# Normalised operands rewritten behind the first product group, second weight parts moved from GpSimd to VectorE, and an instruction planner with a shared port

## The chip, the core and the metric

The kernel runs on one core of a Trainium2 chip. The core has TensorE (matrix products, PE in the profile, with PEld for its weight loads), VectorE (DVE), ScalarE (ACT), GpSimd (POOL) and SyncE (SP), which issues most DMAs. The metric is device time in microseconds: 2119.82 us is the median of three runs before the change (2117.39 to 2120.98). About 0.2% is what a measurement can tell from no change.

## The reference

Everything is float32, with 256 tokens of width 1024. Two blocks of two layers each stand one behind the other.

A layer of the first block is `x += mixer(rms_norm(x))`, then `x += ffn(rms_norm(x))`. Its mixer projects the normalised input into queries, keys, values, gates and a short-convolution branch, runs causal convolutions, evaluates a gated delta rule by chunks (with a triangular solve) in four heads, and projects back. Its feed-forward is `(silu(h Wg) * (h Wu)) Wd` with 2816 hidden columns.

A layer of the second block has three sublayers: feed-forward, token mixer, feed-forward. Each takes

```
rms_norm(x) * gain * (1 + scale) + shift
```

as its input, where scale, shift and an output gate are products of a conditioning vector with `mod_w`, and adds back a gated, normalised result. The token mixer holds a state-space part of 512 channels (a complex scan over time), an attention with forgetting in eight heads, and two sigmoid gates that merge them.

What matters here: each sublayer begins with `rho(t) = 1 / sqrt(mean(x(t)^2) + eps)`, one number for each token, and the first product of `x * gain * rho + shift` with a weight matrix.

## The kernel before, in words

**Layout.** Activations lie transposed: features on the 128 partitions in eight slices (k = 0 to 7), the 256 tokens along the free axis. A product is made at float32 precision from three products of a reduced format: a weight W is cast to a first part `wh` and has a second part `wl = W - wh`, the input likewise `xh` and `xl`, and PSUM gathers `wh xh + wh xl + wl xh` (`group`, line 224, products on line 237). A group is four output slices of 128 columns, eight k-slices and three products each, so 96 products, in four PSUM banks (`pg`, four buffers: the next group's column c has to wait until this group's column c has been read).

**Weights.** They come as a stream of blocks of 128 x 1024 in the order of use (`all_blocks`, `prepare` line 185): SyncE loads one into `wr`, ScalarE or VectorE casts it to `wh` (lines 198, 200), VectorE or GpSimd subtracts `wl` (line 207). A block is two k-slices of a group. Up to four blocks are made ahead. `POOL_SHARE = (1,0,0.56,0)` says which share of the subtractions GpSimd makes, for the stages (first block's mixer, first block's feed-forward, second block's mixer, second block's feed-forward); `HI_SHARE` says the same of casts on VectorE.

**A sublayer.** `pre` (line 345) writes `xh` and `xl` from `x * gain` without rho, so that products can begin before the sum of squares is complete; rho comes later, as a tile of 128 x 256 (line 330 in the first block, line 379 in the second). Every result that leaves PSUM is then multiplied by rho on VectorE (lines 397, 412, 667, 833, 853, 1235, 1328), in the first block's feed-forward a second time on the gate (line 404), and in the first mixer rho is squared and applied to a product (lines 848, 853, 875). In the second block the shift rides along: `xh` has two more columns with the shift vector in two parts, so the `xh` products have 258 columns, and each result column's constant is added up from the two last columns by `shifted` (line 242: VectorE line 245, or ScalarE line 248) and used as a bias.

The feed-forward (`ffn`, line 385) runs six pairs of groups, gate and up, and writes the product of both, split into `ah` and `al`; then the down projection follows in two groups of 22 k-slices. `mixer1` (line 645) runs keys first, then queries, values, and four more groups among the steps of the delta rule (a blockwise solve on lines 783 to 817, where a small product on line 790 alternates with two VectorE steps, 793 and 795). `mixer2` (line 1217) runs `u` first, then seven groups among sixteen pairs of state-space steps (`ssm_pair`, lines 1109 to 1156, on VectorE and GpSimd) and the attention heads.

**GpSimd's other work.** It prepares the state-space tables (`ssm_params`, line 1062), makes three of the eight residual sums at a sublayer's start (lines 570, 571) and multiplies the first two residual slices by `r` ahead of time (`ahead`, line 583; eight slices in the last sublayer). `make` and `ahead` concern the residual of the sublayer's end.

**The order of the work.** The program is written sublayer by sublayer, but what each engine executes is planned: `Order` (line 1549) takes all instructions, gives each an engine, a cost (`price`, line 1583) and dependencies with latencies, lists them by priority in a simulated run (`run`, line 1695), forwards and backwards for several settings, keeps the best list and pins each engine's instructions in its order. In this model engines are independent of one another: a GpSimd instruction and a VectorE instruction run side by side at full speed.

## Time and profile before

| | |
|---|---|
| runs shown (three) | 2117.39, 2119.82, 2120.98 us; median 2119.82 |
| profiled execution, its own time | 2110.74 us |
| its span (first to last instruction) | 2108.9 us |
| TensorE / its weight loads busy | 1929.6 / 1832.8 us (91 / 87%) |
| VectorE busy | 1748.0 us (83%) |
| ScalarE busy | 1044.2 us (50%) |
| GpSimd busy | 654.6 us (31%) |
| mean granted TensorE clock | 0.966 of full speed |
| DMA moved | 391.03 MB, mean 185 GB/s |

The shares are averages over ten sublayers with different limits, so the profile is read by stretches. [...] Matmuls are pipelined and reach into one another, so TensorE's idle time says more than its busy time. An instruction that is held up counts as busy: its duration grows. In a line of the timeline, what stands in brackets is the idle time before it and who ended it.

### The profile page before, as it was taken

What the parts mean: (1) busy time and instruction counts of PE and PEld (TensorE: products, weight loads), DVE (VectorE), ACT (ScalarE), POOL (GpSimd) and SP (SyncE); (2) the same over time, 40 slices, a digit from 0 to 9 for tenths busy, and PEclk for the clock granted to TensorE, in tenths of its full rate; (3) what the DMA queues carried; (4) which work ended last, traced back from release to release, by engine and by line L of the source; (5) the groups of instructions that cost most, each with busy time, mean ns of one, the idle gap of its engine ahead of it and who ended that gap; (6) DMA issues with size and microseconds to landing.
All of it is one profiled execution on the core that took longest, in us unless ns stands there. A gap on an engine that the chain in (4) does not pass through costs nothing. (4 is left out here: it accounts for less than half of the span.)

```text
span 2108.9 us, 38573 instructions
## 1 busy us (share of the span) xinstructions
PE 1929.6 (91%) x14826; PEld 1832.8 (87%) x14826; DVE 1748.0 (83%) x3053; ACT 1044.2 (50%) x1898; POOL 654.6 (31%) x453
## 2 busy tenths in 40 slices
PE   7789999879999998998888879999999888899998
PEld 6789999778999998898666878999999876688997
DVE  8968897887888789977898898877887799977674
ACT  5645644544554555445344454545454534456453
POOL 5532000544300004804666693000000476642000
PEclk9999999989999999999899989999999999999999
DMA  5324777422577777573332546775778432254553
GB/s 200 100 83 139 271 268 283 167 90 91 180 277 272 279 272 250 209 277 125 103 125 80 190 130 209 262 264 187 268 240 280 141 125 90 86 166 145 183 187 120
DMA packets 110248, 391.03 MB, mean 185 GB/s; under 512 B 12912, under 2 KB 13424, under 8 KB 110064
## 3 DMA queue, kind: packets, MB, share of 16 engines
q1 hardware_dynamic: 108336, 382.93, 53.5%
q0 software_dynamic: 1440, 5.24, 0.7%
q8 instruction: 117, 1.92, 0.4%
q14 instruction: 67, 0.55, 0.1%
q10 hardware_dynamic: 288, 0.39, 0.1%
HBM read 383.27 MB, written 1.05 MB: 182 GB/s over the span
## 5 line engine op out<-in xcount | busy, mean ns | idle before, releaser
L237 PE MATMUL g<-xh,wh 128*128 128x258 f32 (+1 forms) x3264 | 933.3, 291 | 42.1 <-DVE xc L667 14.5
L237 PE MATMUL g<-xl,wh 128*128 128x256 f32 x3264 | 934.8, 289 | 10.4 <-DVE xl L360 8.8
L237 PE MATMUL g<-xh,wl 128*128 128x258 f32 (+1 forms) x3264 | 923.7, 288 | 1.7 <-POOL wl L207 0.9
L200 ACT CAST wh<-wr 128x1024 fp32r<-128x1024 f32 (+1 forms) x528 | 550.0, 1046 | 457.3 <-PE g L237 201.5
L207 DVE TENSOR_TENSOR wl<-wr,wh 128x1024 fp32r<-128x1024 f32 (+1 forms) x446 | 575.4, 1298 | 158.8 <-PE g L237 70.2
L237 PEld LDWEIGHTS g<-xh,wh 128*128 128x128 f32 x3264 | 624.6, 193 | 55.5 <-issue 17.2
L237 PEld LDWEIGHTS g<-xl,wh 128*128 128x128 f32 x3264 | 633.1, 194 | 19.0 <-DVE xl L360 11.6
L237 PEld LDWEIGHTS g<-xh,wl 128*128 128x128 f32 x3264 | 627.1, 194 | 5.7 <-issue 3.3
L207 POOL TENSOR_TENSOR wl<-wr,wh 128x1024 fp32r<-128x1024 f32 (+1 forms) x130 | 326.4, 2516 | 642.9 <-PE g L237 239.5
L237 PE MATMUL g<-ah,wh 128*128 128x256 f32 x880 | 249.2, 284 | 3.3 <-DVE act L412 2.5
L237 PE MATMUL g<-ah,wl 128*128 128x256 f32 x880 | 248.1, 283 | 0.0
L237 PE MATMUL g<-al,wh 128*128 128x256 f32 x880 | 247.9, 282 | 0.0
L472 DVE SCALAR_TENSOR_TENSOR mraw<-mraw,siluc 128x1024 f32<-128x1024 f32 x144 | 187.7, 1303 | 20.5 <-DMA mraw<-in_modw 20.0
L237 PEld LDWEIGHTS g<-ah,wh 128*128 128x128 f32 x880 | 166.4, 189 | 3.9 <-issue 3.7
L237 PEld LDWEIGHTS g<-al,wh 128*128 128x128 f32 x880 | 167.0, 190 | 0.0
L237 PEld LDWEIGHTS g<-ah,wl 128*128 128x128 f32 x880 | 165.9, 189 | 0.0
L342 ACT CAST ah<-act 128x256 fp32r<-128x256 f32 x132 | 52.5, 405 | 118.0 <-DVE act L413 93.8
L1109 POOL TENSOR_TENSOR pa<-pa,pb 128x256 f32<-128x256 f32 x96 | 84.6, 897 | 44.2 <-DVE pb L1109 20.6
L1066 POOL COPY stb<-ah 128x1 f32<-128x1 f32 x1 | 0.2, 183 | 224.0 <-ACT ah L342 224.0
L1109 POOL TENSOR_TENSOR pb<-st,stb 128x512 f32<-128x512 f32 x32 | 49.4, 1543 | 56.2 <-DVE st L1134 50.7
L397 DVE TENSOR_TENSOR sg<-g,rho 128x256 f32<-128x256 f32 x132 | 53.9, 420 | 12.6 <-PE g L237 11.2
L1134 DVE TENSOR_TENSOR_SCAN st<-ssm_r,pa 128x128 f32<-128x128 f32 x64 | 63.8, 1015 | 0.2 <-POOL pa L1109 0.2
(451 smaller groups left out, 2749.6 us busy)
## 6 DMA issues: line engine op xcount, KB each, us to landing
wr<-in_wstream SPq DMA_DIRECT2D x568, 512.0 KB, 4.4
mraw<-in_modw SPq DMA_DIRECT2D x144, 512.0 KB, 4.0
stb<-in_ssmb POOLq DMA_DIRECT2D x8, 512.0 KB, 4.7
wr<-in_wstream SPq DMA_DIRECT2D x8, 256.0 KB, 4.5
ux<-gb SPq DMA_DIRECT2D x32, 64.0 KB, 3.2
ux<-gl SPq DMA_DIRECT2D x32, 64.0 KB, 2.4
stb<-in_ssmc POOLq DMA_DIRECT2D x2, 512.0 KB, 5.3
x<-in_x SPq DMA_DIRECT2D x2, 256.0 KB, 4.8
```

The costliest lines, as they stand in the source:

```text
L200: nc.scalar.copy(out=hi[:, :n], in_=raw[:, :n])
L207: e.tensor_tensor(out=lo[:, :n], in0=raw[:, :n], in1=hi[:, :n], op=ALU.subtract)
L237: nc.tensor.matmul(ps[c][:, :x.shape[-1]], wt, x, start=(bi == 0 and k == 0 and i == 0), stop=(bi == len(specs) - 1 and k == n - 1 and i = ...
L342: s.nc.scalar.copy(out=out_h, in_=src)
L397: nc.vector.tensor_tensor(out=a, in0=gp[c][:, :T], in1=rho, op=ALU.mult)
L472: nc.vector.scalar_tensor_tensor(out=w, in0=w, scalar=1.0, in1=s.sc_, op0=ALU.mult, op1=ALU.mult, accum_out=s.mod[l][:, j:j + 1])
L1066: G.tensor_copy(out=flat[:, 0:1], in_=after)
L1109: tt = lambda e, o, a, b, op: e.tensor_tensor(out=o, in0=a, in1=b, op=op)
L1134: scan = lambda i, h, v: V.tensor_tensor_scan(out=st[:, i, h], data0=rb, data1=a4[:, i, h], initial=v, op0=ALU.mult, op1=ALU.add)
```

## The change

It has three parts.

1. **`Input` and `settle`.** `pre` returns an object. The sublayer's first group runs as before with `x * gain` and gets rho (and the shift) on its results. Behind it `settle` rewrites the eight slices of `xh` and `xl` in place with `x * gain * rho + shift`: a product of three on VectorE into `xs` (two buffers), a copy (or an addition of the shift) into `xh` on ScalarE, a subtraction into `xl` on VectorE. All later groups use these, with 256 columns, and their results need no rho and no shift: gates go from PSUM through the activation function on ScalarE, plain results are copied by ScalarE, the up product needs one VectorE instruction. `ahead` is called behind `settle`. In the second block's very first sublayer, where x is scaled by `fing` in place behind `pre`, `settle` uses the plain gains.
2. **`POOL_SHARE = (0,0,0,0)`**: VectorE makes all second parts.
3. **The planner** marks instructions that use a shared port (all of GpSimd's; VectorE's with two wide inputs in SBUF, and copies and scalar operations from SBUF to SBUF) and lets only one of them run at a time; where the port is held, another instruction that needs no port may go first.

```diff
-POOL_SHARE = (1,0,0.56,0)
+POOL_SHARE = (0,0,0,0)
 DEPTH = 2
...
+class Input:
+    def __init__(s, kern, z, gains, shift, xh, xl, rho):
+        s.kern, s.z, s.gains, s.shift, s.xh, s.xl, s.rho = kern, z, gains, shift, xh, xl, rho
+        s.due = True
+    def h(s, k):
+        return s.xh[:, k, :T + 2] if s.due and s.shift is not None else s.xh[:, k, :T]
+    def l(s, k):
+        return s.xl[:, k, :]
+    def settle(s):
+        nc = s.kern.nc
+        s.due = False
+        for k in range(KD):
+            a = s.kern.t(s.kern.misc, [P, T], "xs")
+            nc.vector.scalar_tensor_tensor(out=a, in0=s.z[:, k, :], scalar=s.gains[:, k:k + 1], in1=s.rho,
+                                           op0=ALU.mult, op1=ALU.mult)
+            if s.shift is None:
+                nc.scalar.copy(out=s.xh[:, k, :T], in_=a)
+                nc.vector.tensor_tensor(out=s.xl[:, k, :], in0=a, in1=s.xh[:, k, :T], op=ALU.subtract)
+            else:
+                nc.scalar.activation(out=s.xh[:, k, :T], in_=a, func=AF.Identity, bias=s.shift[:, k:k + 1])
+                nc.vector.scalar_tensor_tensor(out=s.xl[:, k, :], in0=a, scalar=s.shift[:, k:k + 1],
+                                               in1=s.xh[:, k, :T], op0=ALU.add, op1=ALU.subtract)
...
-    def shifted(s, out, ps, scale=1.0):
-        if scale == 1.0:
-            s.nc.vector.tensor_reduce(out=out, in_=ps[:, T:T + 2], axis=mybir.AxisListType.X, op=ALU.add)
-        else:
-            both = s.t(s.misc, [P, 2], "both")
-            s.nc.scalar.activation(out=both, in_=ps[:, T:T + 2], func=AF.Identity, scale=scale, accum_out=out)
+    def shifted(s, out, ps):
+        s.nc.vector.tensor_reduce(out=out, in_=ps[:, T:T + 2], axis=mybir.AxisListType.X, op=ALU.add)
...
         s.make = s.rest = None
-        N = T if shift is None else T + 2
-        return (lambda k: xh[:, k, :N]), (lambda k: xl[:, k, :]), rho, shift is not None
-    def ffn(s, wg, wu, wd, h, done, wg0=0, wu0=0, last=False):
+        return Input(s, z, gains, shift, xh, xl, rho)
+    def ffn(s, wg, wu, wd, h, done, wg0=0, wu0=0, last=False, then=None):
         nc, tc = s.nc, s.tc
-        xh, xl, rho, shift = h
+        rho = h.rho
         with tc.tile_pool(name=s.nm("ffn"), bufs=1, reuse_waits="tile") as pool:
...
                 n = min(4, NF - g0)
-                gp = s.group(wg, [wg0 + (g0 + c) * P for c in range(n)], KD, xh, xl)
+                gp = s.group(wg, [wg0 + (g0 + c) * P for c in range(n)], KD, h.h, h.l)
+                due = h.due
+                if due:
+                    h.settle()
+                    if then:
+                        then()
                 sg = []
...
                     a = s.t(pool, [P, T], "sg", bufs=4)
-                    nc.vector.tensor_tensor(out=a, in0=gp[c][:, :T], in1=rho, op=ALU.mult)
-                    if shift:
-                        cc = s.t(pool, [P, 1], "cc", bufs=4)
-                        s.shifted(cc, gp[c])
-                        nc.scalar.activation(out=a, in_=a, func=AF.Silu, bias=cc)
+                    if not due:
+                        nc.scalar.activation(out=a, in_=gp[c][:, :T], func=AF.Silu)
                     else:
-                        nc.scalar.activation(out=a, in_=a, func=AF.Silu)
-                        nc.vector.tensor_tensor(out=a, in0=a, in1=rho, op=ALU.mult)
+                        nc.vector.tensor_tensor(out=a, in0=gp[c][:, :T], in1=rho, op=ALU.mult)
+                        bias = {}
+                        if h.shift is not None:
+                            cc = s.t(pool, [P, 1], "cc", bufs=4)
+                            s.shifted(cc, gp[c])
+                            bias = {"bias": cc}
+                        nc.scalar.activation(out=a, in_=a, func=AF.Silu, **bias)
                     sg.append(a)
-                up = s.group(wu, [wu0 + (g0 + c) * P for c in range(n)], KD, xh, xl)
+                up = s.group(wu, [wu0 + (g0 + c) * P for c in range(n)], KD, h.h, h.l)
                 for c in range(n):
                     a = s.t(pool, [P, T], "act", bufs=2)
-                    if shift:
-                        cc = s.t(pool, [P, 1], "cc", bufs=4)
-                        s.shifted(cc, up[c])
-                        nc.vector.tensor_tensor(out=a, in0=up[c][:, :T], in1=rho, op=ALU.mult)
-                        nc.vector.scalar_tensor_tensor(out=a, in0=a, scalar=cc, in1=sg[c],
-                                                       op0=ALU.add, op1=ALU.mult)
-                    else:
-                        nc.vector.tensor_tensor(out=a, in0=up[c][:, :T], in1=sg[c], op=ALU.mult)
+                    nc.vector.tensor_tensor(out=a, in0=up[c][:, :T], in1=sg[c], op=ALU.mult)
                     s.split(ah[:, g0 + c, :], al[:, g0 + c, :], a)
...
             if last and i == subs[-1]:
-                s.ahead(True)
                 s.last_gain(s.modG[l][:, i * 8:i * 8 + 8])
-                s.ffn(*w, h, s.last_part, 0, FF, last=True)
+                s.ffn(*w, h, s.last_part, 0, FF, last=True, then=lambda: s.ahead(True))
                 s.last_add(z)
...
             else:
-                s.ahead()
-                s.ffn(*w, h, done, 0, FF)
+                s.ffn(*w, h, done, 0, FF, then=s.ahead)
             z, sq = s.post_add(zn, z)
...
             def conv(g, out):
-                gp = s.group(w, [g * W + c * P for c in range(4)], KD, xh, xl)
+                gp = s.group(w, [g * W + c * P for c in range(4)], KD, h.h, h.l)
+                due = h.due
+                if due:
+                    h.settle()
                 for c in range(4):
...
                     nx[0] += 1
-                    V.tensor_tensor(out=b[:, 3:], in0=gp[c][:, :T], in1=rho, op=ALU.mult)
+                    if due:
+                        V.tensor_tensor(out=b[:, 3:], in0=gp[c][:, :T], in1=rho, op=ALU.mult)
+                    else:
+                        A.copy(out=b[:, 3:], in_=gp[c][:, :T])
                     a = tt([P, T], "cv", 3)
...
             sz = tt([P, 4, T], "sz")
-            zp = s.group(w, [3 * W + c * P for c in range(4)], KD, xh, xl)
+            zp = s.group(w, [3 * W + c * P for c in range(4)], KD, h.h, h.l)
             for c in range(4):
-                a = tt([P, T], "cv", 3)
-                V.tensor_tensor(out=a, in0=zp[c][:, :T], in1=rho, op=ALU.mult)
-                A.activation(out=sz[:, c, :], in_=a, func=AF.Silu)
+                A.activation(out=sz[:, c, :], in_=zp[c][:, :T], func=AF.Silu)
             vb = tt([P, 4, 2, P], "vb")
...
-            rho2 = tt([P, T], "rho2")
-            V.tensor_tensor(out=rho2, in0=rho, in1=rho, op=ALU.mult)
             o = 4 * W + 8
             cs = tt([P, 4, T], "cs")
-            gp = s.group(w, [o + W + c * P for c in range(4)], KD, xh, xl)
+            gp = s.group(w, [o + W + c * P for c in range(4)], KD, h.h, h.l)
             for c in range(4):
-                V.tensor_tensor(out=cs[:, c, :], in0=gp[c][:, :T], in1=rho2, op=ALU.mult)
+                A.copy(out=cs[:, c, :], in_=gp[c][:, :T])
             level(1)
...
                                            op0=ALU.mult, op1=ALU.add)
-                V.tensor_tensor(out=cs[:, c, :], in0=cs[:, c, :], in1=rho, op=ALU.mult)
             level(2)
...
         V, A, G, PE = nc.vector, nc.scalar, nc.gpsimd, nc.tensor
-        xh, xl, rho, _ = h
+        rho = h.rho
         w = ("min", l)
...
-            def proj(cols, sink, scale=1.0):
-                gp = s.group(w, cols, KD, xh, xl)
+            def proj(cols, sink):
+                gp = s.group(w, cols, KD, h.h, h.l)
                 for c in range(len(cols)):
-                    cc = tt([P, 1], "cc", 4)
-                    s.shifted(cc, gp[c], scale)
-                    sink(c, gp[c], cc)
+                    sink(c, gp[c])
             def plain(out):
-                def sink(c, ps, cc):
-                    o = out(c)
-                    V.tensor_tensor(out=o, in0=ps[:, :T], in1=rho, op=ALU.mult)
-                    A.activation(out=o, in_=o, func=AF.Identity, bias=cc)
+                def sink(c, ps):
+                    A.copy(out=out(c), in_=ps[:, :T])
                 return sink
...
             uh = gb.bitcast(F32R)[:, 4:]
-            proj([c * P for c in range(4)], plain(lambda c: u[:, c, :]))
+            gp = s.group(w, [c * P for c in range(4)], KD, h.h, h.l)
+            h.settle()
             for c in range(4):
+                cc = tt([P, 1], "cc", 4)
+                s.shifted(cc, gp[c])
+                V.tensor_tensor(out=u[:, c, :], in0=gp[c][:, :T], in1=rho, op=ALU.mult)
+                A.activation(out=u[:, c, :], in_=u[:, c, :], func=AF.Identity, bias=cc)
                 s.split(uh[:, c, :], gl[:, c, :], u[:, c, :])
...
             def gate(out, c0):
-                def sink(c, ps, cc):
-                    V.tensor_tensor(out=out[:, c0 + c, :], in0=ps[:, :T], in1=rho, op=ALU.mult)
-                    A.activation(out=out[:, c0 + c, :], in_=out[:, c0 + c, :], func=AF.Tanh, scale=0.5, bias=cc)
+                def sink(c, ps):
+                    A.activation(out=out[:, c0 + c, :], in_=ps[:, :T], func=AF.Tanh, scale=0.5)
                 return sink
...
+    def shares(s, e, x):
+        if e == s.POOL:
+            return True
+        if e != s.DVE:
+            return False
+        real = lambda l: [y.bass_ap for y in l if getattr(y, "bass_ap", None) is not None]
+        sbuf = lambda l: [y for y in l if "PSUM" not in str(y.space)]
+        wide = [y for y in sbuf(real(x.ins)) if int(np.prod([n for _, n in list(y.ap)[1:]])) > 1]
+        if len(wide) > 1:
+            return True
+        return len(wide) == 1 and len(sbuf(real(x.outs))) == 1 and str(x.opcode) in ("TensorCopy", "TensorScalarPtr")
...
                     i = k[1]
+            if s.port[i] and held > t:
+                k = min((q for q in avail[e] if not s.port[q[1]]), default=None)
+                if k is not None and k[0] < prio[i] + held - t:
+                    i = k[1]
             avail[e].remove((prio[i], i))
...
             start = t
+            if s.port[i]:
+                start = max(t, held)
+                held = start + s.cost[i]
             if tables and s.sets[i] is not None and now not in s.sets[i]:
```

The remaining lines hand `h.h`, `h.l` and `h.rho` on in place of the functions and the tile, copy results in `mixer1` and `mixer2` in the same way, and carry the port flag through the planner.

## Rows read from the trace of the kernel before

**Rows 1.** Busy us of each engine, by stretch, one for each sublayer.
```profile
core 0: us, PE busy (x) PEld busy (x) DVE busy (x) ACT busy (x) POOL busy (x), PEclk, DMA share, GB/s
7.00:190.00 183.00, 148.77 (x1198) 142.80 (x1198) 155.26 (x302) 103.99 (x264) 87.63 (x37) 0.98 0.38 126
190.00:379.00 189.00, 188.40 (x1585) 188.11 (x1584) 161.11 (x295) 97.40 (x141) 6.01 (x3) 1.00 0.74 259
379.00:562.00 183.00, 152.71 (x1203) 148.68 (x1202) 153.51 (x296) 92.97 (x238) 83.60 (x35) 0.93 0.36 119
...
753.00:968.00 215.00, 200.08 (x1608) 196.29 (x1606) 183.34 (x284) 110.90 (x164) 79.02 (x70) 0.98 0.68 240
968.00:1238.00 270.00, 228.87 (x1528) 195.51 (x1529) 242.13 (x410) 123.96 (x263) 177.83 (x135) 0.92 0.40 130
1238.00:1454.00 216.00, 204.42 (x1612) 201.30 (x1611) 175.10 (x287) 100.97 (x149) 46.46 (x43) 0.95 0.65 219
...
1654.00:1906.00 252.00, 221.71 (x1530) 191.17 (x1529) 226.37 (x402) 118.94 (x255) 146.75 (x105) 0.93 0.37 119
1906.00:2109.00 203.00, 193.33 (x1355) 180.13 (x1354) 130.83 (x230) 95.72 (x140) 14.12 (x14) 0.99 0.50 159
```

**Rows 2.** The waits: engine, line, whom; us in total, times, longest.
```profile
PE m L790 <- DVE w L793: 15.0, 7, 5.2
PE g L237 <- DVE xc L667: 14.5, 5, 5.4
```

**Rows 3.** Busy us of line 207 alone, in two of the mixers.
```profile
7.00:190.00 183.00, 6.42 (x7) 87.38 (x36) 0.98 0.38 126
...
968.00:1238.00 270.00, 41.16 (x25) 67.88 (x27) 0.92 0.40 130
```

**Rows 4.** Line 207: duration ns (min/median/max), first and last start.
```profile
L207 DVE TENSOR_TENSOR wl<-wr,wh x446: 684/1224/3415, 7.0 to 2090.7; 128x1024 fp32r<-128x1024 f32 x147, 128x512 fp32r<-128x512 f32 x2
...
L207 POOL TENSOR_TENSOR wl<-wr,wh x130: 1293/2414/3592, 13.3 to 1891.4; 128x1024 fp32r<-128x1024 f32 x126, 128x512 fp32r<-128x512 f32 x4
```

**Rows 5.** The timeline at 84 us: start us, us, engine, line, operation.
```profile
83.85 2.40 POOL L207 TENSOR_TENSOR wl<-wr,wh 128x1024 fp32r<-128x1024 f32 x1
...
84.46 2.08 DVE L672 SCALAR_TENSOR_TENSOR cv<-xc,pc,cv 128x256 f32<-128x256 f32 x1
```

**Rows 6.** Line 672: durations over the span; then its group in the first mixer.
```profile
L672 DVE SCALAR_TENSOR_TENSOR cv<-xc,pc,cv x72: 468/478/2642, 24.8 to 455.0; 128x256 f32<-128x256 f32 x72
...
L672 DVE SCALAR_TENSOR_TENSOR cv<-xc,pc,cv 128x256 f32<-128x256 f32 x36 | 28.9, 820 | 0.5 <-ACT cv L670 0.3
```

**Rows 7.** The timeline at 196 us: neighbours of one kind, merged.
```profile
195.61 0.88 DVE L360 SCALAR_TENSOR_TENSOR xl<-x,pc,xh 128x256 fp32r<-128x256 f32 x2
...
196.40 2.36 DVE L207 TENSOR_TENSOR wl<-wr,wh 128x1024 fp32r<-128x1024 f32 x2
```

**Rows 8.** The timeline of VectorE at 1923 us, results of a first group.
```profile
1923.27 0.41 DVE L397 TENSOR_TENSOR sg<-g,rho 128x256 f32<-128x256 f32 x1
1923.60 0.14 DVE L245 TENSOR_REDUCE cc<-g 128x1 f32<-128x2 f32 x1
1923.67 0.41 DVE L397 TENSOR_TENSOR sg<-g,rho 128x256 f32<-128x256 f32 x1
```

**Rows 9.** Groups by line: line 413.
```profile
L413 DVE SCALAR_TENSOR_TENSOR act<-act,cc,sg 128x256 f32<-128x256 f32 x88 | 49.2, 572 | 0.3
```

**Rows 10.** The timeline where rho is made, in two feed-forwards.
```profile
198.91 1.75 DVE L330 RECIPROCAL rho<-rho 128x256 f32<-128x256 f32 x1 [0.15 <-ACT rho L329]
202.58 0.19 PEld L237 LDWEIGHTS g<-xh,wh 128*128 128x128 f32 x1
...
1922.27 0.37 ACT L379 COPY rho<-m 128x256 f32<-128x256 f32 x1 [1.52 <-PE m L334]
```

**Rows 11.** Busy us of each engine in two dense stretches.
```profile
220.00:340.00 120.00, 120.00 (x1012) 120.00 (x1011) 105.99 (x203) 60.42 (x88) 0.00 (x0) 1.00 0.80 276
1930.00:2035.00 105.00, 105.00 (x879) 105.00 (x879) 74.49 (x149) 52.60 (x74) 0.00 (x0) 1.00 0.57 181
```

More of the change, by code (lines that the diff above doesn't have):

```diff
@@ L444, in layer1 @@
         if l == DEPTH - 1:
-            s.first_weights(h[2][:, 0:KD])
+            s.first_weights(h.rho[:, 0:KD])
         s.ffn(("fg", l), ("fu", l), ("fd", l), h,
@@ L865, in mixer1 @@
             sw = COLS["scw", l][0]
-            gp = s.group(w, [o + 2 * W + c * P for c in range(4)], KD, xh, xl)
+            gp = s.group(w, [o + 2 * W + c * P for c in range(4)], KD, h.h, h.l)
             for c in range(4):
@@ L932, in mixer1 @@
                     turned(step - 2)
-            gp = s.group(w, [o + c * P for c in range(4)], KD, xh, xl)
+            gp = s.group(w, [o + c * P for c in range(4)], KD, h.h, h.l)
             oh = s.t(s.state, [P, KD, T + 2], "xh", F32R)
@@ L1219, in mixer2 @@
         V, A, G, PE = nc.vector, nc.scalar, nc.gpsimd, nc.tensor
-        xh, xl, rho, _ = h
+        rho = h.rho
         w = ("min", l)
@@ L1338, in mixer2 @@
                         nj += 1
-                    proj([2056 + i * D + (c0 + c) * P for c in range(4)], gate(t, c0), 0.5)
+                    proj([2056 + i * D + (c0 + c) * P for c in range(4)], gate(t, c0))
             GH, GL = (lambda f: gh[:, f, :]), (lambda f: gl[:, f, :])
@@ L1546, in __init__, with node @@
         s.tc = tc
-        s.eng, s.cost, s.sets, s.ins, s.succ, s.npred = [], [], [], [], [], []
+        s.eng, s.cost, s.sets, s.ins, s.succ, s.npred, s.port = [], [], [], [], [], [], []
         s.edges = {}
         s.trace(instructions)
-    def node(s, eng, cost, ins=None, sets=None):
+    def node(s, eng, cost, ins=None, sets=None, port=False):
+        s.port.append(port)
         s.eng.append(eng)
@@ L1650, in trace @@
                 f = str(getattr(x, "func", "")).split(".")[-1]
-                i = end = s.node(e, s.price(e, x), x, s.SETS.get(f) if e == s.ACT else None)
+                i = end = s.node(e, s.price(e, x), x, s.SETS.get(f) if e == s.ACT else None, s.shares(e, x))
             for r in a:
@@ L1703, in run @@
         free, armed, events, now = [0.0] * 7, [1e18] * 7, [], None
-        done = 0
+        done, held = 0, 0.0
         def arm(e, t):
```

1 line of the change is left out of this document (added).

## Prediction

> **What bounds the kernel now.** I read the stages first, as busy time of each engine in ten stretches, one for each sublayer [rows 1]. The reader is to see two kinds. In the feed-forward stretches TensorE is busy nearly all the time: 188.4 of 189 us in the one from 190 us, with VectorE at 161 of 189. In the four mixers (from 7, 379, 968 and 1654 us) TensorE is idle for 34, 30, 41 and 30 us, 136 us together, and VectorE is busy for 85, 84, 90 and 90% of the stretch. Two feed-forward stretches lie between: the one from 753 us leaves TensorE idle for 15 us, the one from 1238 us for 12. The other four hold between 0.6 and 9.7 us (the least and the most stand in the rows, two between are left out).
>
> Next, who lets TensorE wait in a mixer: the waits name VectorE's results, a convolution input for 14.5 us in all and a solver step for 15.0 [rows 2]. So in a mixer VectorE's time is the price, and in a feed-forward stage TensorE's.
>
> Then, why VectorE is busy there. GpSimd makes the second parts of the weights in the mixers: 36 pieces (87.4 us) in the first mixer, 27 (67.9) in the third, and in the second and the fourth much the same, 34 and 27 [rows 3]; a piece takes it 2.41 us against 1.22 on VectorE [rows 4]. The timeline shows what else a piece costs: a convolution step started 0.6 us into GpSimd's piece of 2.40 us and took 2.08 [rows 5]. The same convolution step takes 0.478 in its median instance and 2.642 in its longest [rows 6]. So a VectorE instruction with both inputs in SBUF stands still until GpSimd's piece ends.
>
> **The change, part by part.** The sum is made against the profiled execution's own 2110.7 us; the median of the runs shown is 9.1 us above it (2119.8), and I add that at the end.
>
> *Second parts from GpSimd to VectorE.* First what it frees. In the first mixer the 36 convolution steps have a mean of 0.820 us [rows 6]: (0.820 - 0.478) x 36 = 12.3 us lost in this line alone, which is the lower bound. All of GpSimd's 87.4 us is the upper one. I did the same for every VectorE line, each against its own shortest instance, and got 52 us, 1.45 for each piece; I take this, as the blocked step of [rows 5] lost 1.6. For the second mixer 52 too. In the other two GpSimd also works on the state-space part, and I share the loss out by overlap: 39 and 44 us for the weight pieces. What it adds: two pieces one behind the other take 2.36 us [rows 7], less the overlap of 0.08 that neighbours on VectorE have [rows 8], 1.14 each: 41, 39, 31 and 31 us.
>
> *Multiplications by rho, and shift columns, dropped behind the first group.* A product and a reduction repeat every 0.40 us in the timeline, 0.33 and 0.07 [rows 8]. From the code: a first-block feed-forward loses 40 products (13 us of VectorE), a second-block one 40 products and 40 reductions (16 us), and its 22 three-operand gate products of 0.572 us mean [rows 9] become two-operand ones like those of [rows 8], 0.41 (3 us). A first-type mixer loses 21 products (7 us; 12 become ScalarE copies of some 0.4), a second-type one 28 products and 12 reductions (10 us). In the four TensorE-bound feed-forwards this is worth nothing: VectorE had 28 us free in such a stretch [rows 1].
>
> *The rewriting (settle).* Two times eight VectorE instructions and eight on ScalarE in each of ten stages. Two such rewrites take 0.88 us back to back [rows 7], so 0.40 each, 6.4 us of VectorE a stage; ScalarE's eight copies lie in its idle half. It issues no DMA. GpSimd's early residual products (two, or eight in the last stage) are moved behind it; nothing needs them before the stage's end except the last transposes, so I cost that at nothing. The cover is the length of the stage; if it were gone, eight pieces of about 1.2 us in the last stage are the price.
>
> Net VectorE time in the mixers: -52+41-7+6 = -12, -52+39-7+6 = -14, -39+31-10+6 = -12, -44+31-10+6 = -17. I turn this into stage time at VectorE's busy share, 0.85 to 0.90: **-48 us**. For the two feed-forwards with GpSimd beside them VectorE loses 16+3-6 = 13 us; TensorE's idle 15 and 12 us bound the gain, part of it in front of the first group, where nothing changes: **-8 and -4**.
>
> *The wait that settle adds.* rho is complete about when the first group ends: at 200.66 us in one stage (198.91 + 1.75) with the group's last weights loaded from 202.58, and at 1922.64 in the last stage (1922.27 + 0.37), when the group's products were done [rows 10]. Behind it now stand, for the first slice, a product on VectorE (0.44), a copy on ScalarE (0.4, a copy of this width from PSUM takes it 0.37 [rows 10]) and a subtraction on VectorE (0.44), with handoffs under 2 us, and TensorE's second group waits for them; behind that wait all later groups. VectorE has queued there as well the four results of the first group (1.6 us) and the weight pieces. From below it is nothing where rho leads by over 2 us; from above the whole serial 16 x 0.40 + 1.6 = 8 us. I take 2.5 us in the six feed-forwards, nearer to the lower end since each slice frees 12 products (1.4 us) of TensorE's work, and 1.5 in the mixers, whose VectorE time is counted already: **+21**.
>
> *256 columns instead of 258.* A dense first-block stretch has 1012 products in 120.00 us (118.6 ns), a second-block one 879 in 105.00 (119.5) [rows 11]. 0.9 ns on 3840 products in feed-forwards: **-3**. In the mixers, nothing.
>
> *The listing.* The order of every engine's queue is recomputed with GpSimd and VectorE excluding one another. GpSimd's state-space work stays, and it held VectorE up by some 120 us (the subtraction of above, the other GpSimd lines). No row prices a new order. Two stages with the same work, from 968 and 1654 us, differ by 18 us in today's [rows 1]: that is the bound either way per pair, and -36 where a model that sees the port finds it twice. I take **-12**, a third of it, because the model now sees what delays the queue.
>
> Sum: 2110.7 - 48 - 12 + 21 - 3 - 12 = 2056.7, and 9.1 more: **2066 us**.
>
> [...]
>
> **The rivals.**
>
> *The settle wait decides (slower).* Place: the ten joints behind the first groups. [...] 10 x 8 = 80 in place of 21, and no gain from the listing: 2110.7 - 48 - 12 - 3 + 80 + 9.1 = 2137. It decides from 6.3 us a joint, where the 48, 12 and 3 us are used up. For it: rho is late everywhere, and weight pieces now share VectorE's queue. Against: slices are freed and needed one by one, and the planner ranks them. Chance 0.10. [...]
>
> *The mixers gain nothing.* If their time is the chain of small dependent steps, VectorE's freed time becomes idle time: 2110.7 - 12 - 3 + 21 + 9.1 = 2126. For it: TensorE's waits are for a few long chains. Against: the steps of these chains are the ones that stood 2 us behind GpSimd. Chance 0.11, half of it within 0.2% when the listing gives a few us.
>
> *The mixers run at TensorE's pace.* If the 2 us holds on chain steps were the stages' real limit, half of the 136 us of idle goes, and the clock of 0.92 to 0.98 recovers some: -85 in place of -48 and the listing's -12, and the joints cost 16 with less in the queues: 2110.7 - 85 - 12 - 3 + 16 + 9.1 = 2036. For it: TensorE waits for just the lines that were held. Against: VectorE would then be over 90% busy. Chance 0.22.
>
> That the change doesn't do what it says can nearly be excluded: with all shares at zero no piece reaches GpSimd.
>
> **How the numbers follow.** Forecast 0.57 around 2066, with its own range of 2045 to 2105 (mixers from half to all, listing from +18 to -36 in part). About 0.2%, 4.2 us, can be told from no change. Faster: 0.57 + 0.22 = 0.79; same: 0.06; slower: 0.15. Downwards the range takes in the third rival's 2036 and a little more, 2026; upwards it ends at 2122, where some 0.16 is left out above.
>
> **What would show it.** Right: no GpSimd rows for second parts; convolution steps at 0.48 us mean; the first two mixers at 165 to 175 us and the others near 255 and 235; at each joint a TensorE gap of 1 to 3 us named by the rewritten operands; feed-forwards unchanged to 3 us. Wrong: joints over 5 us, a lower granted clock behind them, mixers within 5 us of today's though VectorE is less busy, or ScalarE, which now empties the gate banks, as what TensorE waits for.

## The result and the profile after

The changed kernel takes 2037.51 us (median of four runs, 2028.72 to 2040.78) beside 2118.61 for the kernel before in the same series; the ratio is 0.962 with an interval of 0.9601 to 0.964. The profiled execution took 2040.2 us, with a span of 2038.4, so it is 70.5 us shorter than the profiled one of before.

The page's first part, for the kernel after: busy time of each engine, its share of the span and its instructions.

```profile
PE 1912.7 (94%) x14826; PEld 1816.3 (89%) x14826; DVE 1630.3 (80%) x2821; ACT 1055.6 (52%) x1935; POOL 348.0 (17%) x323
```

GpSimd lost 306.6 us, VectorE lost 117.7 us although it makes 130 more second parts, and TensorE's busy time fell by 16.9. Where the 70 us went is read from the stretches again, one for each sublayer, with the columns of [rows 1]: the stretch and its length, for each engine the time in which it had an instruction running, with the instructions in brackets, the granted clock as a share of full speed, the DMA engines' busy share and GB/s.

```profile
7.00:165.00 158.00, 144.94 (x1199) 140.80 (x1200) 139.37 (x334) 103.11 (x281) 0.80 (x1) 0.96 0.44 146
165.00:356.00 191.00, 189.93 (x1588) 188.58 (x1589) 154.39 (x274) 98.85 (x149) 0.00 (x0) 1.00 0.75 258
356.00:508.00 152.00, 143.47 (x1198) 139.87 (x1197) 136.78 (x325) 98.68 (x260) 0.31 (x1) 0.98 0.43 143
508.00:703.00 195.00, 190.50 (x1587) 189.75 (x1587) 153.62 (x233) 98.08 (x144) 0.00 (x0) 0.99 0.76 266
703.00:908.00 205.00, 196.63 (x1606) 193.46 (x1606) 173.93 (x223) 112.47 (x173) 80.62 (x68) 0.99 0.72 251
908.00:1167.00 259.00, 225.85 (x1530) 193.60 (x1530) 227.35 (x410) 121.06 (x236) 125.42 (x121) 0.91 0.41 133
1167.00:1384.00 217.00, 201.25 (x1610) 199.03 (x1611) 168.02 (x226) 103.56 (x160) 36.34 (x31) 0.94 0.65 222
...
1584.00:1834.00 250.00, 224.22 (x1531) 191.13 (x1531) 210.06 (x406) 117.67 (x231) 84.90 (x79) 0.90 0.37 120
1834.00:2038.00 204.00, 194.23 (x1354) 180.54 (x1354) 117.70 (x164) 96.31 (x147) 11.78 (x14) 0.98 0.48 156
```

The first block's two mixers went from 183 us each to 158 and 152. TensorE's idle time there is 13 and 9 us in place of 34 and 30. Products overlap: in the first stretch of [rows 11] one lasts 0.281 us on average, and one starts every 0.119. The second block's mixers moved little, 270 to 259 and 252 to 250. The feed-forward with the state-space tables beside it (from 703 us) gained 10. The other feed-forwards are level or a few us longer: 191 for 189, 195 for 191, 217 for 216, 204 for 203.

The convolution step, the line of [rows 6], in the groups by line of the kernel after (line 702 now):

```profile
L702 DVE SCALAR_TENSOR_TENSOR cv<-xc,pc,cv 128x256 f32<-128x256 f32 x72 | 32.3, 479 | 1.8 <-ACT cv L700 1.6
```

Its mean is now 0.479 us, the median of before, and the longest of the 72 takes 0.486: nothing holds this step up any more, where [rows 5] has one at 2.08 us beside a GpSimd piece.

### The profile page after: what moved, and what is told of

It is laid out like the page before. It is cut to its first block, busy times and chain, and to the rows that moved or that the text cites. A ratio compares the mean times of both kernels' runs of the same rounds, so it can differ in the third digit from the quotient of the medians.

```text
span 2038.4 us, 37891 instructions
## 1 busy us (share of the span) xinstructions
PE 1912.7 (94%) x14826; PEld 1816.3 (89%) x14826; DVE 1630.3 (80%) x2821; ACT 1055.6 (52%) x1935; POOL 348.0 (17%) x323
## 5 line engine op out<-in xcount | busy, mean ns | idle before, releaser
L267 PE MATMUL g<-xh,wh 128*128 128x256 f32 (+1 forms) x3264 | 914.3, 288 | 28.7 <-ACT xh L138 7.1
L267 PE MATMUL g<-xl,wh 128*128 128x256 f32 x3264 | 923.6, 287 | 13.8 <-DVE xl L386 12.6
L267 PE MATMUL g<-xh,wl 128*128 128x256 f32 (+1 forms) x3264 | 908.0, 287 | 5.6 <-DVE wl L237 5.5
L237 DVE TENSOR_TENSOR wl<-wr,wh 128x1024 fp32r<-128x1024 f32 (+1 forms) x576 | 727.3, 1271 | 221.1 <-PE g L267 109.8
L267 PEld LDWEIGHTS g<-xh,wh 128*128 128x128 f32 x3264 | 617.7, 192 | 41.8 <-ACT xh L138 11.7
L267 PEld LDWEIGHTS g<-xh,wl 128*128 128x128 f32 x3264 | 620.0, 193 | 9.9 <-DVE wl L237 9.0
L1134 POOL TENSOR_TENSOR pa<-pa,pb 128x256 f32<-128x256 f32 x96 | 100.0, 1059 | 86.4 <-DVE pb L1134 75.2
L369 DVE TENSOR_TENSOR al<-act,ah 128x256 fp32r<-128x256 f32 x132 | 62.7, 500 | 6.9 <-ACT ah L368 5.1
L428 ACT ACTIVATE sg<-g 128x256 f32<-128x256 f32 x108 | 40.3, 385 | 53.5 <-PE g L267 53.2
L441 DVE TENSOR_TENSOR act<-g,sg 128x256 f32<-128x256 f32 x132 | 52.0, 418 | 14.9 <-PE g L267 12.8
```

The source lines that it names most:

```text
L237: e.tensor_tensor(out=lo[:, :n], in0=raw[:, :n], in1=hi[:, :n], op=ALU.subtract)
L267: nc.tensor.matmul(ps[c][:, :x.shape[-1]], wt, x, start=(bi == 0 and k == 0 and i == 0), stop=(bi == len(specs) - 1 and k == n - 1 and i = ...
L369: s.nc.vector.tensor_tensor(out=out_l, in0=src, in1=out_h, op=ALU.subtract)
L428: nc.scalar.activation(out=a, in_=gp[c][:, :T], func=AF.Silu)
L441: nc.vector.tensor_tensor(out=a, in0=up[c][:, :T], in1=sg[c], op=ALU.mult)
L1134: tt = lambda e, o, a, b, op: e.tensor_tensor(out=o, in0=a, in1=b, op=op)
```

## The experiments

The change has three parts, so they were taken one and two at a time. Below, "share" is `POOL_SHARE`, "operands" the rewriting with all that hangs on it, and "listing" the port in the planner. "Port" is the planner's word for what two instructions may not hold at once; what the trace of before shows is the holding. A product of two SBUF tiles on line 1109 (`pa<-st,stb`) takes 0.679 us at its shortest, 1.456 in the median and 1.761 at its longest, while the one of the same size that reads PSUM (`pa<-m,stb`) stays between 0.659 and 0.693. A cast from SBUF to SBUF on line 198, 0.686 us in the median, took 2.84 at 542.18, beside a GpSimd piece that ran from 542.08 to 544.46. Where the edit is one of these, the diff ahead of the prediction is the edit, and only its first lines are given again. Stage lengths in the tables go from a stage's first product in the trace to the next stage's; they come from one profiled execution each. M1 and M2 are the mixers of the first and second block, F1 their feed-forwards in the first block, and F2a to F2d the four of the second; two numbers are the two layers.

### The share alone

```diff
-POOL_SHARE = (1,0,0.56,0)
+POOL_SHARE = (0,0,0,0)
```

> The kernel before with one line changed: no GpSimd share of second parts in any stage. Port theory (GpSimd's pieces hold VectorE up, which is what bounds the first block's mixers): most of the 81 us comes back with this line alone, 2050 to 2080 us, with the first two mixers at 155 to 170 us instead of 184 and 183. Listing theory (the gain is the planner's knowledge of the port): little alone, 2095 to 2125 us. Operand theory (fewer VectorE results per group): VectorE then has 130 pieces more and nothing less, so 2120 to 2160 us.

Measured: 2019.88 us, ratio 0.9555 (0.9534 to 0.9576). One line gives 96 us, more than the whole change and more than the port theory allowed, and the intervals of the two ratios do not touch. The stretches of the two first-block mixers and of the second block's, in this kernel:

```profile
7.00:167.00 160.00, 146.50 (x1201) 143.28 (x1201) 140.40 (x341) 97.41 (x261) 0.33 (x1) 0.96 0.44 146
...
356.00:506.00 150.00, 142.68 (x1200) 140.51 (x1200) 135.55 (x330) 90.88 (x237) 0.31 (x1) 0.99 0.43 144
...
917.00:1169.00 252.00, 220.54 (x1531) 189.97 (x1531) 229.94 (x430) 122.86 (x260) 125.92 (x127) 0.94 0.41 138
...
1580.00:1816.00 236.00, 216.76 (x1530) 187.25 (x1530) 209.71 (x429) 119.26 (x255) 81.56 (x78) 0.96 0.39 129
```

VectorE is busy for 140.4 and 135.6 us in the first two, 15 and 18 less than in [rows 1], though it does 36 and 34 subtractions more. The stages became 23 and 33 us shorter, more than VectorE was relieved: its idle time fell too, by 8 and 15 us, and TensorE's by 21 and 23. In the second stage TensorE's busy time fell by another 10 us, with a granted clock of 0.99 in place of 0.93. The waits say part of why. Of this kernel, TensorE's waits for the two results of [rows 2]:

```profile
PE g L281 <- DVE xc L667: 3.0, 1, 3.0
PE m L790 <- DVE w L793: 2.2, 2, 1.4
```

The solver's small product on line 790 waited 15.0 us in seven places before, 2.2 in two now; the convolution input goes from 14.5 to 3.0, and it is another product that waits. The step that the waits name, line 793, reads PSUM and never took more than 0.283 us before. What was held up is the other step of the same chain, line 795, which has both inputs in SBUF: it took 0.247 us in the median before and 2.357 at its longest. Its group before and in the share alone:

```profile
L795 DVE TENSOR_TENSOR V<-V,w 128x120 f32<-128x120 f32 (+14 forms) x30 | 20.0, 668 | 0.4
L795 DVE TENSOR_TENSOR V<-V,w 128x120 f32<-128x120 f32 (+14 forms) x30 | 6.7, 222 | 0.3
```

From its first product on line 790 to its last step on line 795 the solver took 24.9 and 28.5 us before, in the two layers, and takes 20.1 and 19.0 here, 14 us less for 13.3 us of holding. This chain of short dependent steps paid for steps that came while a GpSimd piece ran: before, the one at 96.94 us took 2.16, beside two pieces that ran from 96.39 to 101.34. That accounts for a quarter of the 56 us; the other chains were not followed step by step. A simpler reason, that GpSimd's slower pieces came too late for TensorE, falls: in the kernel before, TensorE's products waited for one of them for 0.9 us in all.

### The listing alone, and the operands alone

```diff
+            if s.port[i]:
+                start = max(t, held)
+                held = start + s.cost[i]
...
```

> The kernel before with the port in the planner alone; GpSimd keeps its share of second parts and every result its multiplication by rho. Port theory: GpSimd's 310 us of pieces in the mixers still exclude VectorE, the planner can only place them better: 2085 to 2115 us. Listing theory: 2040 to 2070 us, first two mixers at 155 to 165. Operand theory: within 0.5% of before, 2108 to 2128 us.

Measured: 2109.07 us, ratio 0.9972 (0.995 to 0.9994), so 6 to 7 us for a planner with the port in its model while GpSimd keeps its pieces. The ranges of the port theory and of the operand theory both hold it, and a gain of this size can be the list's own (below). The first two mixers come to 177 and 168 us, where the share alone brings them to 160 and 150.

```diff
+                due = h.due
+                if due:
+                    h.settle()
...
```

> The kernel before with the rewritten operands alone; GpSimd's share and the old planner stay. Port theory: the rewriting adds 16 two-input VectorE instructions a stage that GpSimd's pieces can hold up, and a wait at each of ten joints; what is dropped read PSUM and was not held: 2110 to 2150 us. Listing theory: the same. Operand theory: 2050 to 2080 us.

Measured: 2143.76 us, ratio 1.0127 (1.0096 to 1.0158): slower by 28 us, as the port and the listing theory expected. With GpSimd's pieces in place, the rewriting's own product is held up too: of this kernel, the groups on VectorE of the first block's rewriting,

```profile
L132 DVE SCALAR_TENSOR_TENSOR xs<-x,pc,rho 128x256 f32<-128x256 f32 x32 | 22.6, 726 | 0.1
L136 DVE TENSOR_TENSOR xl<-xs,xh 128x256 fp32r<-128x256 f32 x32 | 17.0, 555 | 0.3
```

against 0.479 us for the first in the kernel after (shown below). That is 8 us for the 32 products. The products that it replaces read PSUM; those of line 667 took 0.416 us on average in the kernel before, and 0.426 at most, with GpSimd's pieces beside them.

### Two parts at a time

Share and listing, without the operands:

> Share and planner without the rewritten operands. Port theory: all that the share gives and a little from the state-space stages, 2030 to 2060 us, and no joint gaps: if the joints cost what the trace of after shows (48 us of TensorE idle time around the ten joints, 14 before), this is as fast as the change or faster, 2015 to 2045. Listing theory: 2040 to 2060. Operand theory: clearly slower than the change, 2080 us or more.

Measured: 2041.02 us, ratio 0.9653 (0.9627 to 0.968). The port theory and the listing theory both allowed this; the operand theory did not.

Share and operands, without the listing:

> The change without the port in the planner. Port theory: the first two mixers hold no GpSimd piece any more, so the old planner is right there; only the state-space stages lose: 2040 to 2065 us. Listing theory: 2080 us or more. Operand theory: 2035 to 2050 us.

Measured: 2024.08 us, ratio 0.9583 (0.9552 to 0.9613), faster than any of the three theories expected: the second block's mixers, which were to lose without the port in the planner, are shorter than in the change.

Listing and operands, with GpSimd's old share:

> The change with GpSimd's old share of second parts (all in the first block's mixers, 0.56 in the second's). Port theory: the first two mixers go back to 175 us or more and the whole to 2085 to 2120 us. Listing theory: 2040 to 2065 us. Operand theory: 2040 to 2070 us.

Measured: 2124.74 us, ratio 1.0049 (1.0028 to 1.0071), 5 us above the port theory's range and far above the other two.

All eight corners, in us (medians; the kernel before was between 2115.4 and 2118.6 in the four series):

| | old planner | port in the planner |
|---|---|---|
| GpSimd's share kept, old operands | 2116 | 2109 |
| GpSimd's share kept, rewritten operands | 2144 | 2125 |
| share at zero, old operands | 2020 | 2041 |
| share at zero, rewritten operands | 2024 | 2038 (the change) |

The share is worth 68 to 120 us in every pair. The listing gives 7 and 19 us while the share is kept and costs 21 and 13 us once it is gone. The operands cost 28 and 16 with the share, 4 at share zero with the old planner, and give 3 with the new one. So the operand theory falls, the listing theory falls, and the share alone brings 96 us and the other two parts, put on top of it, take back 18. The differences of 3, 4 and 7 us are no larger than what another list of the same work makes (below).

Stage lengths in us, of the traces:

| | M1 | F1 | F2a | M2 | F2b, F2c, F2d |
|---|---|---|---|---|---|
| before | 184, 183 | 189, 190 | 215 | 270, 253 | 215, 200, 202 |
| listing alone | 177, 168 | 194, 191 | 212 | 284, 266 | 212, 200, 204 |
| operands alone | 195, 188 | 192, 197 | 211 | 274, 261 | 216, 202, 204 |
| listing, operands | 177, 172 | 192, 197 | 210 | 286, 261 | 215, 203, 205 |
| share alone | 160, 150 | 189, 191 | 220 | 252, 237 | 213, 198, 203 |
| share, listing | 160, 152 | 191, 190 | 204 | 276, 245 | 212, 197, 201 |
| share, operands | 160, 153 | 190, 195 | 213 | 243, 240 | 216, 200, 203 |
| the change | 158, 153 | 191, 195 | 205 | 259, 250 | 216, 200, 205 |

With the share at zero the listing shortens F2a, where GpSimd builds its tables, by 8 and 16 us and lengthens the second block's mixers by 9 to 24 us a layer. With the share kept it lengthens three of the four second-block mixers too, by 12 to 14 us; what it gives there comes from the first block's mixers, 6 to 18 us a layer. The operands shorten F2a without it, and lengthen most of the other feed-forwards.

### What a list is worth by itself

Any edit gives another list, so two kernels were run with one number of the planner's priorities moved.

```diff
-MIXP = 0.1
+MIXP = 0.12
```

In the share alone:

> The kernel before with the share at zero and one number of the planner's priorities moved from 0.10 to 0.12: another list of the same work. It measures what a list is worth by itself. If lists of the same model differ by little, this is within 8 us of share_alone, 2012 to 2028 us; if the lists are a lottery, it may be 2000 or 2045.

Measured: 2028.14 us, ratio 0.9576 (0.9558 to 0.9595), 8 us above share_alone, at the edge of what was expected. One mixer is 246 us instead of 237.

In share and listing:

> Share and port in the planner, with the same number moved. If the port in the planner costs time in the second block's mixers as such, this is 2030 to 2055 us, with mixers of 260 us or more and 243 or more; if share_and_listing had a bad draw, it is near share_alone, 2010 to 2028, with mixers near 250 and 236.

Measured: 2036.59 us, ratio 0.9618 (0.9599 to 0.9638). The mixers take 258 and 252 us, against 252 and 237 or 248 and 246 without the port. So the direction of the listing's loss holds in both draws (21 and 8 us), but a draw is worth 4 to 8 us in the whole and up to 19 in a stage; differences of that size between two kernels here prove nothing.

### Why the listing costs

```diff
-            if s.port[i] and held > t:
-                k = min((q for q in avail[e] if not s.port[q[1]]), default=None)
-                if k is not None and k[0] < prio[i] + held - t:
-                    i = k[1]
```

> Share and port in the planner, without the rule by which an instruction that needs no port goes first; the waiting time of the port stays in the model. If that rule is what spoils the second block's mixers, they come back to about 252 and 237 us and the whole to 2005 to 2025 us; if it is the port's waiting itself, which makes the planner give the state-space steps more room, 2035 to 2060.

Measured, on share and listing: 2053.38 us, ratio 0.9691 (0.9669 to 0.9714). It is worse without the rule, with the mixers at 274 and 264 us, so the rule does not spoil them; the port's waiting in the model does, or what the search makes of it. The stretch of the first M2 with share and listing, to be held against 917 to 1169 of the share alone above:

```profile
903.00:1180.00 277.00, 236.07 (x1532) 199.04 (x1533) 227.06 (x434) 124.37 (x261) 116.17 (x118) 0.89 0.38 126
```

VectorE is busy for 3 us less, TensorE idle for 41 us in place of 31, and the granted clock 0.89 in place of 0.94. TensorE's longest waits there are no longer those of the state-space steps but of the projections and gates:

```profile
PE g L237 <- ACT xh L359: 5.7, 3, 2.3
PE g L237 <- DVE pa L1358: 5.5, 1, 5.5
PE g L237 <- DVE gb L1328: 5.4, 3, 2.9
```

The holding itself is not gone either. In the second block's mixers VectorE makes a product of two SBUF tiles (`pa<-st,stb`, line 1109 or 1134) that takes 0.68 us at its shortest in the kernels before and after. Its mean is 1.20 us in the share alone and 1.40 with the listing, and 0.95 in the change. That the planner gives up more for the port than the holding costs is what this looks like. Why its search ends there is open.

### GpSimd's share in the second block's mixers alone

```diff
-POOL_SHARE = (0,0,0,0)
+POOL_SHARE = (0,0,0.56,0)
```

> The change, but GpSimd keeps 0.56 of the second parts in the second block's mixer. Port theory: there GpSimd's pieces exclude VectorE as before, but the planner places them: 5 to 20 us slower than the change, 2042 to 2060. If a piece is worth more beside the state-space steps than it blocks: 2020 to 2037 us. First two mixers as in the change, 155 us.

Measured, on the kernel after: 2077.85 us, ratio 0.9838 (0.9804 to 0.9872); it costs 40 us, twice what the port theory allowed. The mixers take 281 and 260 us against 259 and 250, and F2a and the rest are as in the change. Of the 87 us that the share is worth beside the other two parts (2125 to 2038), the second block's mixers thus account for some 40 by the medians, and for 32 by the stages of the two traces.

### The rewriting behind the second group

```diff
-                if due:
-                    h.settle()
-                    if then:
-                        then()
                 sg = []
...
                 up = s.group(wu, [wu0 + (g0 + c) * P for c in range(n)], KD, h.h, h.l)
+                if due:
+                    h.settle()
+                    if then:
+                        then()
```

In the mixers likewise, behind queries or values; the second group's results get rho and shift.

> The change with the rewriting moved behind the second group of each stage, whose results get rho and shift as the first's do. If the joint costs because rho comes when the first group ends, it now has a group's time of slack: the TensorE idle time around the joints falls from 48 us towards the 14 of before, and the time by 15 to 30 us, 2005 to 2025. If the joint is VectorE's throughput, the same work stands one group later and nothing is won, 2030 to 2045 us.

Measured: 2043.46 us, ratio 0.9664 (0.9633 to 0.9696): no gain. The stages say more than the time. F1, F2b, F2c and F2d are 188, 192, 213, 198 and 204 us, together 13 less than in the change and as long as in the share alone: there the joint did cost, and a group's time of slack takes that away. The first block's mixers, the first M2 and F2a give it back, with 163, 154, 267 and 210 us; the second M2, 246, is 4 shorter. That may be one of the planner's draws; it isn't settled.

The joint itself, in the change's second F1. VectorE's timeline there (start, us, engine, line, operation):

```profile
517.66 1.75 DVE L356 RECIPROCAL rho<-rho 128x256 f32<-128x256 f32 x1 [0.47 <-ACT rho L355]
519.33 1.16 DVE L237 TENSOR_TENSOR wl<-wr,wh 128x1024 fp32r<-128x1024 f32 x1
520.41 1.21 DVE L497 SCALAR_TENSOR_TENSOR mraw<-mraw,siluc 128x1024 f32<-128x1024 f32 x1
521.55 0.08 DVE L497 DVE_READ_ACCUMULATOR mraw<-mraw,siluc 128x1 f32 x1
521.55 0.48 DVE L132 SCALAR_TENSOR_TENSOR xs<-x,pc,rho 128x256 f32<-128x256 f32 x1
521.95 1.22 DVE L237 TENSOR_TENSOR wl<-wr,wh 128x1024 fp32r<-128x1024 f32 x1
523.08 0.42 DVE L136 TENSOR_TENSOR xl<-xs,xh 128x256 fp32r<-128x256 f32 x1
523.41 0.88 DVE L132 SCALAR_TENSOR_TENSOR xs<-x,pc,rho 128x256 f32<-128x256 f32 x2
524.21 0.42 DVE L430 TENSOR_TENSOR sg<-g,rho 128x256 f32<-128x256 f32 x1
```

ScalarE's first copy there:

```profile
522.06 0.41 ACT L135 CAST xh<-xs 128x256 fp32r<-128x256 f32 x1
```

And TensorE's:

```profile
520.88 0.29 PE L267 MATMUL g<-xh,wl 128*128 128x256 f32 x1
524.77 0.36 PE L267 MATMUL g<-xh,wh 128*128 128x256 f32 x1 [3.60 <-ACT xh L135]
```

rho was complete at 519.41, 1.8 us ahead of the first group's end at 521.17, so here rho was not late. A weight piece and a modulation product were put in front of the rewriting, another piece into the middle of the first slice, and TensorE stood for 3.6 us. The trace puts that wait down to ScalarE's copy, but the first slice was copied by 522.47 and its second part was there by 523.50. The next group also has to wait until the first group's first result has been read from its PSUM bank, and that product on line 430 stood in VectorE's queue behind all of the above and ended at 524.63; TensorE went on at 524.77. So it is the order of VectorE's queue that cost here.

### Casts moved to ScalarE

```diff
-HI_SHARE = (0.55,0.05,0,0)
+HI_SHARE = (0.25,0.05,0,0)
```

On the share alone:

> The share at zero and, in the first block's mixers, a quarter instead of 0.55 of the casts on VectorE: some 12 casts of 0.69 us a mixer leave VectorE (140 of 160 us busy) and 12 of 1.05 go to ScalarE (97 of 160). If VectorE's time still sets these two stages, each gets 5 to 8 us shorter, 2004 to 2012 us; if chains and TensorE set them now (idle for 14 and 7 us), nothing or a little more, 2015 to 2030.

Measured: 2013.72 us, ratio 0.9511 (0.9493 to 0.9529), the fastest kernel of this study, 24 us faster than the change. The two stretches:

```profile
7.00:163.00 156.00, 145.78 (x1201) 142.14 (x1202) 134.38 (x329) 111.96 (x277) 0.51 (x1) 0.97 0.45 150
352.00:502.00 150.00, 144.68 (x1201) 141.85 (x1199) 131.52 (x321) 102.99 (x251) 0.31 (x1) 0.98 0.44 150
```

VectorE got 6 and 4 us, the stages 4 and nothing: TensorE is idle for only 10 and 5 us here, so VectorE's time no longer sets the second of these stages. The time lies between the two ranges that were expected. Of the 6 us against the share alone the rest lies in F2a (215 for 220), which the edit doesn't touch, and is of the size of a draw. Whether the casts as such make it faster than the share alone is thus not shown beyond the first mixer; that both beat the change is.

## Why the prediction came out as it did

The time lies in the stated range, but 29 us below the forecast of 2066 and below the 2045 to 2105 that went with it. It is within 2 us of the third rival, "the mixers run at TensorE's pace", which had 0.22. The sign and the cause, GpSimd's pieces holding up VectorE, were right. Several terms were not, and two errors offset each other in part: the mixers' term was too small, the listing's had the wrong sign.

The third rival's mechanism is what the share alone shows: TensorE's idle time in the four mixers goes from 136 to 72 us, about half as it says, and the mixers gain 91 us for its 85. That the change's time agrees with it to 2 us is luck, since the rival counted no loss by the listing.

**Second parts to VectorE: the cause right, the turning into stage time mis-sized.** The 52 us of holding were nearly right: by the share alone, VectorE's busy time fell by 15 and 18 us while 41 and 39 us of pieces came to it, so 56 and 57 had been lost. I expected VectorE to be relieved by 12 and 14 us in the first block's mixers; it was by 16 and 17 (155.26 to 139.37, 153.51 to 136.78). The step that failed is the next one: "I turn this into stage time at VectorE's busy share, 0.85 to 0.90". For these two that meant 22 us; the stages got 25 and 31 shorter, 56 together. The share alone shows it without the other parts, 23 and 33 us for 15 and 18. Multiplying by the busy share takes it that VectorE's idle time grows by what is left; there it fell by 8 and 15 us. Held steps stood in chains that other engines wait for too, the solver's among them, and the granted clock of the second mixer rose as well, from 0.93 to 0.99. [rows 2] had named the solver's chain, though not by the line that was held, and was then left out of the sum.

**The second block's mixers.** Predicted 26 us less from this term; the share alone gives 18 and 16 by the traces, the change 11 and 3. By the pairs above the difference is the listing.

**The listing: wrong in sign.** I took -12 with bounds of -36 and +18, "because the model now sees what delays the queue". With the share at zero it costs 8 to 21 us in the three pairs that were run, at the upper bound. With the share kept the time comes out as the term says, -7 and -19, but by the first block's mixers, where GpSimd's pieces are. I had argued it from the 120 us of holding by the state-space work, which stays; in the mixers that have it, the port in the planner cost time in seven of the eight pairs of stages in the table.

**The joints: size about right for the feed-forwards, far too small for the mixers.** I had 2.5 us for each feed-forward and 1.5 in a mixer. In the change's trace TensorE's gaps behind the first groups are 0, 3.6, 1.6, 6.5, 1.9 and 0.6 us in the feed-forwards, 14 for the 15 that I had, and 10.7, 7.1, 5.1 and 5.0 in the mixers, 28 for 6. In the mixers it is not the rewritten operands that TensorE waits for. It is a narrow product on line 307, whose small weight tiles VectorE writes on lines 299 and 304 (0.2 us each); these stand in its queue among the rewriting and the weight pieces:

```profile
PE g L307 <- DVE sqb L299: 14.8, 2, 7.7
PE g L307 <- DVE sqb L304: 10.1, 2, 5.1
```

The same product waits for 6.1 and 3.0 us in the first block's mixers of the share alone, so 19 of the 28 us are new. F1, F2b, F2c and F2d are together 10 us longer with share and operands than with the share alone (five stages, 2 us each). F2a is 7 us shorter by the same pair, perhaps by the 40 products and 40 reductions dropped, perhaps by the draw. In the first M1 the rewriting runs from 22.80 to 35.3 us, among weight pieces and casts, and TensorE's next main group starts at 34.4, 13 us behind the first one's end, but the stage isn't longer for it than with the share alone. The sign of being wrong, joints over 5 us with a lower granted clock behind them, thus came at five of the ten joints: the clock is 0.57 from 22 to 36 us, 0.50 from 1189 to 1202, around the 6.5 us, and around the other three 0.76 (368 to 382), 0.68 (920 to 936) and 0.79 (1596 to 1612). The rival that this wait decides takes the upper bound of 8 us at each joint and would have needed 6.3; the ten come to 42 us, and it falls.

**The two feed-forwards with GpSimd beside them.** Predicted -8 and -4. F2a gained 10, but share and listing without the dropped products has 204 us there, so the reason given isn't shown; F2b is level, 216 for 215.

The rewriting's own prices were about right. Of the kernel after:

```profile
L132 DVE SCALAR_TENSOR_TENSOR xs<-x,pc,rho 128x256 f32<-128x256 f32 x32 | 14.4, 479 | 0.0
L135 ACT CAST xh<-xs 128x256 fp32r<-128x256 f32 x32 | 12.4, 401 | 12.6 <-DVE xs L132 11.1 <-DVE xc L695 1.5
```

**256 columns.** Predicted -3 on 3840 products. A dense stretch of the third second-block feed-forward after:

```profile
1430.00:1520.00 90.00, 90.00 (x760) 90.00 (x760) 66.75 (x100) 45.19 (x65) 0.00 (x0) 1.00 0.79 277
```

90.00 us for 760 products are 118.4 ns, 1.1 less than in [rows 11]: 4 us by that count.

**The mixers gain nothing** (the rival with 0.11) falls with the first table. **The overlap on VectorE.** The joint's timeline above shows a weight piece of 1.16 us starting at 519.33 with the next instruction at 520.41, 0.08 before the piece's end, so the overlap of 0.08 that the prediction counted is there after the change too.

## What to carry to other kernels

An engine whose instructions hold up those of the busy one isn't free capacity. Here a convolution step of 0.478 us took 2.08 beside a GpSimd piece; taking 130 pieces of 2.41 us off a GpSimd that was 31% busy, and giving them to a VectorE that was 83% busy, made this kernel 96 us faster, 88 in the other draw. Where an engine's rows have a mean far above their median, as line 795 has with 0.668 us against 0.247, look at which chains these rows stand in before converting busy time into stage time. And of a change in three parts, run each part alone: here one line was faster than all three together.

## What was not expected of the hardware

That VectorE's busy time falls while it takes GpSimd's work over had been forecast, 155 to 140 us in the first mixer with 36 pieces more: instructions held count as busy (2.08 us for a step of 0.478), and a VectorE that looks 85% full had room for 41 us of pieces. Not expected was that its idle time would fall with it. And the lower granted clock came with the longer gaps: the first M2 with TensorE idle for 31 us ran at 0.94 in the share alone, with 41 us at 0.89 with share and listing. TensorE's busy time there rose from 221 to 236 us for the same products, so about 16 of the 25 us between the two lists are busy time that came with the lower clock.
